# Second MLP products of six hidden blocks in sixteen as seven block products in place of eight (Strassen's scheme), weights staged in half pieces

## The chip, the cores and the metric

The kernel runs on one core of a Trainium2 chip. The metric is the device time of one execution in microseconds (us), the median of several runs. Engines are named as in the profile: PE (TensorE) multiplies, PEld loads the matrix that stands still into it, DVE (VectorE) and ACT (ScalarE) do arithmetic, POOL (GpSimd) and SP (SyncE) here mostly start DMAs or idle.

## The reference

A decoder trunk of two layers on 256 tokens of width 1024, float32 in and out. Layer 0 has stick-breaking attention, layer 1 native sparse attention with keys and values from the stream after layer 0; each is followed by a squared-ReLU MLP with a hidden width of 4096, and at the end stands an RMSNorm.

```python
def sqrelu_mlp(x, w1, w2):
    h = jax.nn.relu(x @ w1)
    return (h * h) @ w2
...
for layer in range(DEPTH):
    hn = rms_norm(h, norm_gain[layer, 0])
    ... # attention, added to h
    h = h + sqrelu_mlp(rms_norm(h, norm_gain[layer, 1]), mlp_w1[layer], mlp_w2[layer])
return rms_norm(h, final_norm)
```

## The kernel before

**Precision.** Every product of float32 numbers is made of three: each operand is split into a high part (fp32r, a cast) and a low part (the number less its high part), and high by high, high by low and low by high are added up in PSUM. `mm3` (L361) issues the three matmuls, `mm` (L355) one of them. For weights ACT makes the high part `wh` (L301) and DVE the low part `wl` (L307), in `split`.

**Weights.** All weights come in one fixed list, `feed` (L205) and `feed_mlp` (L214), in pieces of 128x2048 (1 MB), into three raw buffers. `fetch` (L255) issues a piece's DMA on SP as soon as a buffer's last reader, DVE's `wl`, is placed. Each piece is split in two halves of 1024 columns into one of three pairs wh, wl. `W` asks for a piece, `gone` gives it back.

**The MLP** (`mlp`, L465) cuts the hidden width of 4096 into 16 blocks of 256, one piece of w1 and one of w2 each. The hidden tile of a block stands with the hidden numbers on the partitions, so it has four quarters of 128x128: two halves f of the hidden numbers by two halves t of the tokens.
- First product (`first`): for each f, eight matmuls of 512 columns (wh against the tokens' high and low parts side by side) and eight of 256 (wl against the high part), into a PSUM bank `pu`. ACT copies the 256 columns of the cross product out (`mr`, L507), DVE adds the other 256 (`mu`, L508).
- `square`: DVE makes relu(u) u (`ms`, L520), ACT its high part `hh` (L521), DVE its low part `hl` (L522).
- Second product (`second`, `piece`): for each of the two column halves n of the output and the two token halves t, two quarters by three matmuls of 512 columns, which add to one of four banks `acc` over all 16 blocks. Eight products of a quarter with a 128x512 piece of w2 a block, thus 24 matmuls.

The second products of block c - 2 follow the first products of block c. Two pairs of `pu` banks alternate, so eight banks are in use: four acc, four pu. The last two blocks are worked off by (t, n) instead; as each output quarter ends, DVE scales it and adds it to the residual `hres` (`res`, L451 and L453), and `finish` (L1421) squares, scales (ACT L1433, DVE L1435), applies the gain (L1440) and writes it out (L1436). The order of (t, n) in layer 1 is (0,0), (0,1), (1,0), (1,1), and the very last quarter is done in two parts of 256 columns, the second into a bank of its own, `accz`.

**The order of work** is not written down by hand. PE's order follows the program, and a planner (`Order`, L41, with `Chain`) keeps a clock by cost formulas (`act` L159, `dve` L163, `pool` L167) and a rank for each chain of steps; ACT's and DVE's instructions are placed where their engine would be free by that clock, so that each engine then works through its own fixed list.

Of the kernel before, what the change touches and what calls it, by code (L numbers as in the profile page):

```python
# [8 lines left out]
F32 = mybir.dt.float32  # L9
# [6 lines left out]
P = 128  # L16
# [11 lines left out]
V_CUT = ((1, 1), (2, 1), (3, 1), (4, 2), (6, 2))  # L28
# [92 lines left out]
class Chain:  # L121
# [29 lines left out]
    def hurry(self):  # L151
        if self.rank > 0:
            for x in self.o.ready:
                if x[3] == self.one:
                    x[0] = 0
            self.rank = 0
# [15 lines left out]
def hybrid_kernel(ctx, tc, x, xt, eye, gcols, gfin, wqk, wv, wo0, wkv, wvs, wq, wg, wo1, w1, w2, cw1, cw2, cpos, gate_b, consts, out):  # L172
# [29 lines left out]
    NB = 3  # L202
    stream = []

    def feed(src, n, whole=False):  # L205
        stream.append((src, n, whole))
        return len(stream) - 1

    i_v0 = [feed(wv[:, n * 512:(n + 1) * 512], 512) for n in range(2)]
    i_v = [feed(wv[:, k * D:(k + m) * D], m * D) for k, m in V_CUT]  # L210
    i_qk = [feed(wqk[p], 2048) for p in range(NP)]
    i_o0 = [[feed(wo0[n, i], 2048) for n in range(2)] for i in range(2)]

    def feed_mlp(layer):  # L214
        wa, wb = [], []
        for c in range(NFC):
            wa.append(feed(w1[layer, c], 2048))
            if c >= 2:
                wb.append(feed(w2[layer, c - 2], 2048))
        return wa, wb + [feed(w2[layer, c], 2048) for c in (NFC - 2, NFC - 1)]  # L220

    i_m = [feed_mlp(0)]
    i_kv = [[feed(wkv[n, i], 2048) for i in range(2)] for n in range(2)]
# [3 lines left out]
    def feed_cw(n):  # L227
        c, i = divmod(n, 2)
        i_c[c][i] = feed(cw1[c, i], 2048, True)

    feed_cw(0)
    i_q.append(feed(wq[0], 2048))
    feed_cw(1)
    feed_cw(2)
    i_q.append(feed(wq[1], 2048))
    feed_cw(3)
    i_vs.append(feed(wvs[0], 2048))
    i_q.append(feed(wq[2], 2048))
    i_vs.append(feed(wvs[1], 2048))
    i_q.append(feed(wq[3], 2048))  # L240
    i_o1 = [[feed(wo1[n, i], 2048) for n in range(2)] for i in range(2)]
    i_m.append(feed_mlp(1))

    class Weights:
        raws, made, parts, gone, cur, landed, path, pool = [], [], [], 0, -1, 0.0, 0.0, None

    ws = Weights()
    ways = {"hi": "A"}

# [5 lines left out]
    def fetch():  # L255
        j = len(ws.raws)
        if j == len(stream):
            return
        src, n, whole = stream[j]
        if j in i_v0 or j in i_v:  # L260
            raw = ws.pool.tile([P, n], F32, name=f"rv{j}", bufs=1)
        else:
            raw = wp.tile([P, n], F32, tag="raw", name="raw", bufs=3)
        ws.raws.append(raw)
        ws.made.append(None)
        cuts = 2 if j in (0, 2) or j in i_v[-2:] else 1
# [3 lines left out]
        for h in range(2):  # L270
            if h < cuts:
                lands(P * n * 4 // cuts)
            ws.parts.append(Chain(o, whole_part(j, h) if whole else split(j, h), rank_of(j), ws.landed))

    def rank_of(j):
        return (0.5, 2, 4)[min(2, max(0, j - ws.cur))]

    def whole_part(j, half):
        if 2 * j + half:
            yield ws.his[2 * j + half - 1]  # L280
        ws.his[2 * j + half].finish()

    def split(j, half):
        n = stream[j][1]
        if 2 * j + half:
            yield ws.his[2 * j + half - 1]
        before = [i for i in range(j) if not stream[i][2]]
        while len(before) >= NB and ws.gone <= before[-NB]:
            w = Waiter()
            ws.waiting.append(w)  # L290
            yield w
        ws.parts[2 * j + half].rank = rank_of(j)
        r = slice(half * n // 2, (half + 1) * n // 2)

        def hi(e):
            def f():
                if ws.made[j] is None:
                    ws.made[j] = (wp.tile([P, n], F32R, tag="wh", name="wh", bufs=NB),
                                  wp.tile([P, n], F32R, tag="wl", name="wl", bufs=NB))
                if e == "A":  # L300
                    nc.scalar.copy(ws.made[j][0][:, r], ws.raws[j][:, r])  # L301
                else:
                    nc.vector.tensor_copy(ws.made[j][0][:, r], ws.raws[j][:, r])
            return f

        def lo():
            nc.vector.tensor_sub(ws.made[j][1][:, r], ws.raws[j][:, r], f32(ws.made[j][0][:, r]))  # L307

        m = n // 2
        k = {"A": (195 + 0.835 * m, hi("A"), False), "D": (200 + 0.49 * m, hi("D"), True)}  # L310
        yield {e: k[e] for e in ways["hi"]}
        ws.his[2 * j + half].finish()
        yield {"D": (150 + 1.045 * m, lo, True)}
        if half and j > i_v[-1]:
            fetch()

    class Waiter(Chain):
# [8 lines left out]
        def hurry(self):  # L326
            pass

    ws.his = [Waiter() for _ in range(2 * len(stream))]
    ws.waiting = []  # L330

    def W(i, half=None):
        ws.cur = max(ws.cur, i)
        while 2 * i + 1 >= len(ws.parts):
            o.run(o.run(o.t))
        for h in range(2) if half is None else (half,):
            for q in range(2 * i + h + 1):
                if not ws.parts[q].done:
                    ws.parts[q].hurry()
            o.need(ws.parts[2 * i + h])  # L340
        return ws.raws[i] if stream[i][2] else ws.made[i]

    def gone(i):
        assert ws.gone == i, (ws.gone, i)
        ws.gone += 1
        if stream[i][2]:
            fetch()
# [107 lines left out]
    def out_part(oT, acc, idx, n, kks, chains=(), ts=range(T)):  # L455
        for k in kks:
            i, kk = divmod(k, 4)
            w = W(idx[i][n], kk // 2)
            o.need(*chains)
            for t in ts:  # L460
                mm3(acc[n][t], tok(oT, k, t), cut(w, kk * 512, (kk + 1) * 512), k == 0, k == NK - 1)
# [3 lines left out]
    def mlp(layer, gi, x_, ch, pt, rs, pus, accs, mid, ends, ap):  # L465

        wa, wb = i_m[layer]
        acc = [[None, None], [None, None]]
        held = []
        r2 = [None, None]  # L470

        def piece(c, hT, t, n, q=(0, 512)):
            o.need(hT[2])
            for f in range(2):
                w = W(wb[c], f)
                if c == 0 and f == 0:
                    acc[n][t] = B(accs[2 * n + t], f"acc{t}{n}")
                mm3(acc[n][t][:, q[0]:q[1]], tok(hT, f, t), cut(w, f * D + n * 512 + q[0], f * D + n * 512 + q[1]),
                    f == 0 and (c == 0 or q[0] > 0), c == NFC - 1 and f == 1)

        def second(c, hT):
            for n in range(2):
                for t in range(T):
                    piece(c, hT, t, n)
            gone(wb[c])

        def begin(c):
            return ([B(pus[c % 2][f], f"pu{f}") for f in range(2)],
                    [ap.tile([P, 512], F32, name=m) for m in ("mr", "mu", "ms")], [])
# [1069 lines left out]
```

## Time and profile before

| | |
|---|---|
| median of 3 runs | 619.59 us (619.07 to 620.25) |
| profiled execution | 619.5 us |
| its span in the profile | 617.7 us |
| PE busy | 609.4 us, 99% of the span |
| DVE, ACT, POOL busy | 421.0, 330.0, 40.7 us |
| bytes by DMA | 108.26 MB, mean 175 GB/s |

The profiled execution's time is its span and 1.8 us around it. A busy share says how much of the span an engine had an instruction under way; matmuls are pipelined, so their listed durations overlap and can add up to more than the stretch they fill. The chain that ended last is followed back from the last instruction, at each step to what released it.

### The profile page before, as it was taken

What the parts mean: (1) busy time and instruction counts of PE and PEld (TensorE: products, weight loads), DVE (VectorE), ACT (ScalarE), POOL (GpSimd) and SP (SyncE); (2) the same over time, 40 slices, a digit from 0 to 9 for tenths busy, and PEclk for the clock granted to TensorE, in tenths of its full rate; (3) what the DMA queues carried; (4) which work ended last, traced back from release to release, by engine and by line L of the source; (5) the groups of instructions that cost most, each with busy time, mean ns of one, the idle gap of its engine ahead of it and who ended that gap; (6) DMA issues with size and microseconds to landing.
All of it is one profiled execution on the core that took longest, in us unless ns stands there. A gap on an engine that the chain in (4) does not pass through costs nothing.

```text
span 617.7 us, 8966 instructions
## 1 busy us (share of the span) xinstructions
PE 609.4 (99%) x3580; PEld 515.1 (83%) x3580; DVE 421.0 (68%) x609; ACT 330.0 (53%) x563; POOL 40.7 (7%) x57
## 2 busy tenths in 40 slices
PE   9999999999999999999999999999999999999995
PEld 6899988888888888888887788777888888888884
DVE  6668896676656566655938999664876665566645
ACT  6757674464555444443805876553653555434432
POOL 0000000000000000000111444310000000000001
PEclk9999999999999999999999999999999999999998
DMA  8973315264555545555355525212465455554501
GB/s 323 350 294 147 137 69 204 73 240 175 198 201 204 188 164 198 200 202 197 141 200 204 205 74 202 69 69 103 146 239 189 177 204 204 179 189 179 203 1 68
DMA packets 18042, 108.26 MB, mean 175 GB/s; under 512 B 2384, under 2 KB 3664, under 8 KB 5968
## 3 DMA queue, kind: packets, MB, share of 16 engines
q1 hardware_dynamic: 17424, 107.07, 47.4%
q8 instruction: 28, 0.46, 0.3%
q10 hardware_dynamic: 576, 0.62, 0.3%
q14 instruction: 14, 0.11, 0.0%
HBM read 106.63 MB, written 1.05 MB: 174 GB/s over the span
## 4 chain that ended last, share of the span: by engine, by line
PE 95%; DMA 2%; ACT 1%; issue 1%; DVE 1%; POOL 0%; POOLq 0%; DVEq 0%; ACTq 0%
PE acc L355 35%; PE pu L355 29%; PE qk L355 8%; PE pk L355 5%; PE pv L355 4%; PE po L355 3%; PE z L355 3%; PE qp L355 3%; PE ptp L367 2%; DMA raw<-in_wq 1%; PE ph L355 1%; PE pt L367 1%; PE pa L367 1%; DMA xraw<-in_xt 1%; ACT pe L1093 0%
## 5 line engine op out<-in xcount | busy, mean ns | idle before, releaser
L307 DVE TENSOR_TENSOR wl<-raw,wh 128x1024 fp32r<-128x1024 f32 x180 | 216.1, 1221 | 105.0 <-ACT wh L301 105.0
L301 ACT CAST wh<-raw 128x1024 fp32r<-128x1024 f32 x180 | 184.7, 1052 | 108.4 <-PE acc L355 45.9
L355 PE MATMUL pu<-xn,wh 128*128 128x512 f32 x512 | 129.7, 392 | 0.0
L355 PEld LDWEIGHTS pu<-xn,wh 128*128 128x128 f32 x512 | 93.3, 188 | 18.0 <-issue 0.5
L355 PE MATMUL acc<-wh,hh 128*128 128x512 f32 (+1 forms) x256 | 99.8, 390 | 0.0
L355 PE MATMUL acc<-wl,hh 128*128 128x512 f32 (+1 forms) x256 | 99.7, 390 | 0.0
L355 PE MATMUL acc<-wh,hl 128*128 128x512 f32 (+1 forms) x256 | 99.4, 388 | 0.0
L355 PEld LDWEIGHTS pu<-xn,wl 128*128 128x128 f32 x512 | 70.9, 190 | 5.7
L355 PE MATMUL pu<-xn,wl 128*128 128x256 f32 x512 | 72.6, 282 | 0.0
L355 PEld LDWEIGHTS acc<-wh,hl 128*128 128x128 f32 x256 | 48.1, 188 | 10.1
L355 PEld LDWEIGHTS acc<-wh,hh 128*128 128x128 f32 x256 | 48.2, 188 | 9.2
L355 PEld LDWEIGHTS acc<-wl,hh 128*128 128x128 f32 x256 | 48.2, 188 | 8.8
L521 ACT CAST hh<-ms 128x512 fp32r<-128x512 f32 x32 | 19.9, 621 | 61.3 <-DVE ms L520 61.3
L355 PE MATMUL qk<-xa,wh 128*128 128x256 f32 x256 | 47.3, 286 | 0.0
L355 PE MATMUL acc<-wh,oT 128*128 128x512 f32 x128 | 43.6, 403 | 0.0
L355 PEld LDWEIGHTS qk<-xa,wh 128*128 128x128 f32 x256 | 39.8, 192 | 0.5 <-issue 0.3
L507 ACT COPY mr<-pu 128x256 f32<-128x256 f32 x64 | 23.6, 369 | 23.8 <-PE pu L355 23.8
L355 PE MATMUL qk<-xa,wl 128*128 128x256 f32 x128 | 36.2, 283 | 0.0
L522 DVE TENSOR_TENSOR hl<-ms,hh 128x512 fp32r<-128x512 f32 x32 | 22.1, 691 | 19.4 <-ACT hh L521 19.4
L355 PE MATMUL pk<-wh,xk 128*128 128x512 f32 (+1 forms) x128 | 33.6, 342 | 0.0
L1093 ACT ACTIVATE pe<-z,nm 128x256 f32<-128x256 f32 (+1 forms) x64 | 26.2, 427 | 10.7 <-DVE nm L1099 10.7
L355 PEld LDWEIGHTS acc<-wh,oT 128*128 128x128 f32 x128 | 24.0, 188 | 5.6 <-issue 0.7
(181 smaller groups left out, 750.9 us busy)
## 6 DMA issues: line engine op xcount, KB each, us to landing
raw<-in_w SPq DMA_DIRECT2D x64, 1024.0 KB, 4.8
raw<-in_wqk SPq DMA_DIRECT2D x8, 1024.0 KB, 4.9
raw<-in_wo SPq DMA_DIRECT2D x8, 1024.0 KB, 4.8
raw<-in_wkv SPq DMA_DIRECT2D x4, 1024.0 KB, 4.8
raw<-in_cw SPq DMA_DIRECT2D x4, 1024.0 KB, 5.0
raw<-in_wq SPq DMA_DIRECT2D x4, 1024.0 KB, 5.4
rv<-in_wv SPq DMA_DIRECT2D x6, 512.0 KB, 7.5
raw<-in_wvs SPq DMA_DIRECT2D x2, 1024.0 KB, 5.2
```

Of the source, the lines that this page charges most:

```text
L301: nc.scalar.copy(ws.made[j][0][:, r], ws.raws[j][:, r])
L307: nc.vector.tensor_sub(ws.made[j][1][:, r], ws.raws[j][:, r], f32(ws.made[j][0][:, r]))
L355: nc.tensor.matmul(o_, a, b, start=first, stop=last, skip_group_check=True)
L367: nc.tensor.transpose(o_, a, i)
L507: yield act(256, lambda: nc.scalar.copy(r[:, q], pu[f][:, 256:512]))
L521: yield act(512, lambda: nc.scalar.copy(hh, sv))
L522: yield dve(512, lambda: nc.vector.tensor_sub(hl, sv, f32(hh)), port=True)
L1093: return act(n, lambda: nc.scalar.activation(d, z, AF.Exp, bias=nm[:, i:i + 1], accum_out=rs[:, t, hd, b:b + 1]), 150)
```

## The change

In blocks 2, 4, 6, 8, 10 and 12 of both layers (`FAST`) the second product is a 2x2 block product by Strassen's scheme: seven products of 128x512, each of three matmuls, in place of eight. They add to seven banks: four that stay the outputs' own, to which the plain blocks add as well, and three more for products 1, 6 and 7. In return the other blocks use the same four outputs by changed terms: the bank of output (t=0, n=1) holds the difference to another output (quarters E2 and S3), and product 5's bank is added to two outputs at the end. What comes with it:

- Sums of quarters of the hidden tile (E2, S1 to S4), on DVE; `hh` and `hl` then hold six or eight quarters. Sums of weights (`ty`, kinds "a" and "b"), made by DVE from two raw half pieces; ACT makes their high part `th` and DVE their low part `tl`.
- Weight pieces are halves: 128x1024 (512 KB), in six raw buffers and six pairs wh, wl, and four pairs th, tl. w1 and w2 are laid out by halves in memory (`first`, `second` in the layout function).
- Three acc banks more leave one pu bank from block 4 on: both halves of every first product use it in turn. ACT copies all 512 columns out of it (`mu`, L630 after), and DVE adds the two parts in one instruction from there (`ms`, L645). The last block's second half uses product 7's bank, which is empty again by then.
- After block 12 `gather` adds the three extra banks to `hres`: two copies on ACT, two sums and four updates on DVE.
- From block 4 to 14 the two halves of a second product stand apart: first product half 0, second product half 0 (products 1, 3, 5, 7), first product half 1, second product half 1 (products 2, 6, 4).
- The last two blocks run in the order (0,0), (1,0), (1,1), (0,1) in layer 0 and (0,0), (1,1), (0,1), (1,0) in layer 1.

```diff
-V_CUT = ((1, 1), (2, 1), (3, 1), (4, 2), (6, 2))
+FAST = ((2, 4, 6, 8, 10, 12),) * 2
...
-    NB = 3
+    H = 1024
+    NR, NB, NT = 6, 6, 4
...
+        def two(c, wide):
+            s = [w2[layer, c][:, h * H:(h + 1) * H] for h in range(2)]
+            fast = c in FAST[layer]
+            x = feed(s[0], H)
+            if fast:
+                loads.append((s[1], H, 1, False))
+                ls = [len(loads) - 2, len(loads) - 1]
+                a = item("a", H, ls)
+            if wide:
+                one(c + 2, 1)
+            if fast:
+                y = item("w", 512, ls[1:])
+                wb.append([x, y, a, item("b", H, ls)])
+            else:
+                wb.append([x, feed(s[1], H)])
...
+            yield dve(H, lambda: nc.vector.tensor_add(
+                ty, x.rearrange("p (a q) -> p a q", a=2), y[:, 512:H][:, None, :].to_broadcast([P, 2, 512])), port=True)
+        else:
...
+            yield dve(512, lambda: nc.vector.tensor_add(ty[:, 0], t0[:, 1], x[:, 0:512]), port=True)
+            yield dve(512, lambda: nc.vector.tensor_add(ty[:, 1], ty[:, 0], y[:, 0:512]), port=True)
...
+        ws.made[i] = hi, lo = [ws.tp.tile([P, H], F32R, name=t, bufs=NT) for t in ("th", "tl")]
+        yield cast(H, hi, ty)
+        ws.his[off].finish()
+        yield {"D": (150 + 1.045 * H, lambda: nc.vector.tensor_sub(lo, ty, f32(hi)), True)}
...
+        banks = {1: extra[0], 2: accs[0], 3: accs[2], 4: accs[1], 5: accs[3], 6: extra[1], 7: extra[2]}
...
+        def half(c, hT, h):
+            if c in fast:
+                x, y, a, b = wb[c]
+                if h == 0:
+                    term(1, hT, A11, x, 0)
+                    term(3, hT, S4, x, 1)
+                    gone(x)
+                    term(5, hT, S1, a, 0)
+                    term(7, hT, S3, a, 1)
+                    gone(a)
+                else:
+                    term(2, hT, A12, y, 0)
+                    gone(y)
+                    term(6, hT, S2, b, 0)
+                    term(4, hT, A22, b, 1)
+                    gone(b)
+            else:
+                for a, m, n in ((A11, 2, 0), (A21, 4, 0), (A22, 5, 1), (E2, 3, 1)) if h == 0 else (
+                        (A12, 2, 0), (A22, 4, 0), (A21, 5, 1), (S3, 3, 1)):
+                    term(m, hT, a, wb[c][h], n)
+                gone(wb[c][h])
...
+            if k0 == 0 and c >= 4:
+                if free[0] is not None:
+                    o.need(free[0])
+                pu[f] = B(extra[2] if f and c == NFC - 1 else pus[1][1], "pu")
...
-                    yield act(256, lambda: nc.scalar.copy(r[:, q], pu[f][:, 256:512]))
-                    yield dve(256, lambda: nc.vector.tensor_add(u[:, q], pu[f][:, 0:256], r[:, q]))
+                    yield act(512, lambda: nc.scalar.copy(u[:, f, :], pu[f]))
...
+                yield dve(512, lambda: nc.vector.tensor_add(s4, u4[:, :, 0], u4[:, :, 1]), port=True)
...
+                yield dve(256, lambda: nc.vector.tensor_sub(s[:, 4:6], s[:, 2::-2], s[:, 3:0:-2]), port=True)
+                if c in fast:
+                    yield dve(256, lambda: nc.vector.tensor_sub(s[:, 6:8], s[:, 1:5:3], s[:, 3:6:2]), port=True)
+                    yield dve(128, lambda: nc.vector.tensor_sub(s[:, 8], s[:, 6], s[:, 0]), port=True)
+                    yield from parts(5, 9, 4)
...
+            apart = 4 <= c < NFC - 1
+            first(c, st, 0, 0, NK)
+            if apart:
+                half(*held[0], 0)
+            first(c, st, 1, 0, NK)
+            held.append((c, square(c, st)))
+            if not apart:
+                half(*held[0], 0)
+            half(*held.pop(0), 1)
```

On PE a block of layer 0's MLP before: the first product in two banks, then 24 matmuls into the four acc banks (the first three are shown).

```order
L355 MATMUL pu0_1513<-xn_1169,wh_1432 128x512 x8
L355 MATMUL pu0_1513<-xn_1169,wl_1433 128x256 x8
L355 MATMUL pu1_1514<-xn_1169,wh_1432 128x512 x8
L355 MATMUL pu1_1514<-xn_1169,wl_1433 128x256 x8
L355 MATMUL acc00_1387<-wh_1476,hh_1382 128x512
L355 MATMUL acc00_1387<-wl_1477,hh_1382 128x512
L355 MATMUL acc00_1387<-wh_1476,hl_1383 128x512
```

On PE the second half of a first product and of a fast block's second product after it, in the same layer: one bank `pu` (2089, then 2131 for the next half), and nine matmuls between.

```order
L443 MATMUL pu_2089<-xn_1235,wh_1962 128x512 x8
L443 MATMUL pu_2089<-xn_1235,wl_1963 128x256 x8
L443 MATMUL acc2_1469<-wh_1979,hh_1912 128x512
L443 MATMUL acc2_1469<-wl_1980,hh_1912 128x512
L443 MATMUL acc2_1469<-wh_1979,hl_1913 128x512
L443 MATMUL acc6_1702<-th_2028,hh_1912 128x512
L443 MATMUL acc6_1702<-tl_2029,hh_1912 128x512
L443 MATMUL acc6_1702<-th_2028,hl_1913 128x512
L443 MATMUL acc4_1476<-th_2028,hh_1912 128x512
L443 MATMUL acc4_1476<-tl_2029,hh_1912 128x512
L443 MATMUL acc4_1476<-th_2028,hl_1913 128x512
L443 MATMUL pu_2131<-xn_1235,wh_2040 128x512 x8
```

What moved: the next first product's half now follows after nine matmuls into other banks and takes the bank that the last one filled; `th` and `tl` are the weight sums' parts.

On ACT around a block of layer 0 before: the copies out of PSUM (`mr`), the weight casts and the cast of the hidden tile.

```order
L301 CAST wh_1962<-raw_1860 128x1024 x2
L507 COPY mr_1959<-pu0_1957 128x256
L301 CAST wh_2006<-raw_1904 128x1024
L507 COPY mr_1959<-pu1_1958 128x256
L301 CAST wh_2006<-raw_1904 128x1024
L521 CAST hh_2004<-ms_1961 128x512
```

On ACT after, around the same place on PE: `mu_1271<-pu_2089` is the copy that empties the bank before pu_2131 can be filled.

```order
L630 COPY mu_1271<-pu_2034 128x512
L356 CAST wh_2068<-raw_1936 128x1024
L356 CAST wh_2081<-raw_2022 128x1024
L356 CAST wh_2113<-raw_2024 128x1024
L630 COPY mu_1271<-pu_2089 128x512
L356 CAST wh_2122<-raw_2026 128x1024
L356 CAST th_2148<-ty_2138 128x1024
L630 COPY mu_1271<-pu_2131 128x512
L650 CAST hh_2111<-ms_2033 128x512
```

What moved: a cast of a weight half (`wh_2113`) still stands right ahead of a copy, but what the copy sets free is now the only bank. 

On DVE the kernel's end before, from the last whole quarter's update of hres to the last scaling.

```order
L1440 SCALAR_TENSOR_TENSOR ys0_4112<-hres0_72,gf_4108 128x512
L453 SCALAR_TENSOR_TENSOR hres1_73<-acc10_4312,r2_4720,hres1_73 128x512
L1435 TENSOR_SCALAR ys0_4112<-ys0_4112,ssq0_4110 128x704
L1440 SCALAR_TENSOR_TENSOR ys1_4113<-hres1_73,gf_4108 128x512
L1451 TENSOR_SCALAR ssq1_4111<-ssq1_4111 128x1
L453 SCALAR_TENSOR_TENSOR hres1_73<-acc11_4331,r2_4720,hres1_73 128x256 x2
L453 SCALAR_TENSOR_TENSOR hres1_73<-accz_5531,r2_4720,hres1_73 128x256
L1451 TENSOR_SCALAR ssq1_4111<-ssq1_4111 128x1
L1440 SCALAR_TENSOR_TENSOR ys1_4113<-hres1_73,gf_4108 128x256
L1451 TENSOR_SCALAR ssq1_4111<-ssq1_4111 128x1
L1440 SCALAR_TENSOR_TENSOR ys1_4113<-hres1_73,gf_4108 128x256
L1435 TENSOR_SCALAR ys1_4113<-ys1_4113,ssq1_4111 128x704
```

On DVE the same end after.

```order
L541 SCALAR_TENSOR_TENSOR hres0_72<-acc3_4675,r2_4935,hres0_72 128x512
L1634 TENSOR_SCALAR ssq0_4452<-ssq0_4452 128x1
L541 SCALAR_TENSOR_TENSOR hres1_73<-acc4_4664,r2_4993,hres1_73 128x256
L1622 SCALAR_TENSOR_TENSOR ys_4454<-hres0_72,gf_4450 128x512
L541 SCALAR_TENSOR_TENSOR hres1_73<-acc4_4664,r2_4993,hres1_73 128x256
L1617 TENSOR_SCALAR ys_4454<-ys_4454,ssq0_4452 128x704
L541 SCALAR_TENSOR_TENSOR hres1_73<-accz_6067,r2_4993,hres1_73 128x256
L1634 TENSOR_SCALAR ssq1_4453<-ssq1_4453 128x1
L1622 SCALAR_TENSOR_TENSOR ys_4454<-hres1_73,gf_4450 128x256
L1634 TENSOR_SCALAR ssq1_4453<-ssq1_4453 128x1
L1622 SCALAR_TENSOR_TENSOR ys_4454<-hres1_73,gf_4450 128x256
L1617 TENSOR_SCALAR ys_4454<-ys_4454,ssq1_4453 128x704
```

What moved: token half 0's gain and scaling (`ys<-hres0`) now stand between the updates of the last quarter; before, that half was through ahead of them.

## Rows read from the trace of the kernel before

**Rows 1.** The page of the profile, busy time, share of the span and count of each engine, and the shares of the span by engine in the chain that ended last.

```profile
PE 609.4 (99%) x3580; PEld 515.1 (83%) x3580; DVE 421.0 (68%) x609; ACT 330.0 (53%) x563; POOL 40.7 (7%) x57
...
PE 95%; DMA 2%; ACT 1%; issue 1%; DVE 1%; POOL 0%; POOLq 0%; DVEq 0%; ACTq 0%
```

**Rows 2.** The chain that ended last in order of time, inside the first MLP. Columns: start in us from the span's start, duration in us, engine, tile written, line, count.

```profile
154.61 5.47 PE acc L355 x24
160.08 5.56 PE pu L355 x32
165.64 5.47 PE acc L355 x24
```

**Rows 3.** The table by stretches. Columns: the stretch in us, its length, then for PE, PEld, DVE, ACT and POOL the busy time (and instructions), the granted clock of PE as a share of full speed, the mean busy share of the DMA engines, GB/s. The first two are most of the first and of the second MLP, the third two whole blocks.

```profile
154.60:275.90 121.30, 121.30 (x618) 103.66 (x617) 74.12 (x92) 59.75 (x82) 0.00 (x0) 1.00 0.54 191
451.00:594.40 143.40, 143.40 (x730) 122.55 (x729) 88.03 (x109) 70.28 (x96) 0.00 (x0) 1.00 0.51 184
206.97:229.03 22.06, 22.06 (x113) 18.85 (x113) 13.37 (x17) 10.53 (x14) 0.00 (x0) 1.00 0.54 191
```

**Rows 4.** The timeline of PE over one first product. Columns: start, duration, engine, line, operation, tiles out<-in, shape, count.

```profile
137.86 1.98 PE L355 MATMUL pu<-xn,wh 128*128 128x512 f32 x8
139.68 1.11 PE L355 MATMUL pu<-xn,wl 128*128 128x256 f32 x8
140.63 2.00 PE L355 MATMUL pu<-xn,wh 128*128 128x512 f32 x8
142.47 1.12 PE L355 MATMUL pu<-xn,wl 128*128 128x256 f32 x8
...
143.42 0.40 PE L355 MATMUL acc<-wh,hh 128*128 128x512 f32 x1
```

**Rows 5.** The timeline of DVE in the first MLP. Columns as above, and in brackets the idle time ahead of an instruction and what ended it.

```profile
127.42 0.68 DVE L520 SCALAR_TENSOR_TENSOR ms<-mu 128x512 f32<-128x512 f32 x1
128.02 0.74 DVE L508 TENSOR_TENSOR mu<-pu,mr 128x256 f32<-128x256 f32 x2
...
205.35 2.36 DVE L307 TENSOR_TENSOR wl<-raw,wh 128x1024 fp32r<-128x1024 f32 x2 [1.75 <-ACT wh L301]
...
211.09 0.42 DVE L508 TENSOR_TENSOR mu<-pu,mr 128x256 f32<-128x256 f32 x1
211.43 1.22 DVE L307 TENSOR_TENSOR wl<-raw,wh 128x1024 fp32r<-128x1024 f32 x1
212.56 0.69 DVE L520 SCALAR_TENSOR_TENSOR ms<-mu 128x512 f32<-128x512 f32 x1
...
213.94 0.69 DVE L522 TENSOR_TENSOR hl<-ms,hh 128x512 fp32r<-128x512 f32 x1 [0.69 <-ACT hh L521]
```

**Rows 6.** ACT: the timeline in the first MLP; then, from the groups of instructions by line and shape, the copies of 512 columns out of PSUM (busy us, mean ns of one; idle us ahead and what ended it); then the timeline of one such copy and of the matmul that it let start.

```profile
140.88 0.37 ACT L507 COPY mr<-pu 128x256 f32<-128x256 f32 x1 [0.78 <-PE pu L355]
...
142.71 1.05 ACT L301 CAST wh<-raw 128x1024 fp32r<-128x1024 f32 x1 [1.46 <-PE pu L355]
143.67 0.37 ACT L507 COPY mr<-pu 128x256 f32<-128x256 f32 x1
...
147.17 0.62 ACT L521 CAST hh<-ms 128x512 fp32r<-128x512 f32 x1 [2.19 <-DVE ms L520]
...
L1146 ACT COPY pT<-ptp 128x512 f32<-128x512 f32 x12 | 7.1, 594 | 1.8 <-PE ptp L367 1.7
...
348.07 0.60 ACT L1146 COPY pT<-ptp 128x512 f32<-128x512 f32 x1
...
348.73 0.66 PE L367 MATMUL ptp<-ident,pe 128*128 128x128 f32 x4 [0.28 <-ACT pT L1146]
```

**Rows 7.** DMA: the stretch at the kernel's start, in columns as in the table by stretches above; the page's DMA issues (count, KB each, median us from issue to landing); and the issuing instructions of the weights' tile on SP (shortest, median and longest ns, first and last start in us).

```profile
0.00:27.40 27.40, 26.47 (x110) 19.92 (x111) 16.71 (x30) 17.46 (x26) 2.33 (x12) 1.00 0.93 356
...
raw<-in_w SPq DMA_DIRECT2D x64, 1024.0 KB, 4.8
...
raw<-in_wq SPq DMA_DIRECT2D x4, 1024.0 KB, 5.4
...
L269 SPq DMA_DIRECT2D raw<-in_w x64: 327/328/328, 85.1 to 581.3; - x64
```

**Rows 8.** The timeline of the kernel's end, DVE, PE and the last DMA issue on ACT's queue.

```profile
605.32 0.75 DVE L453 SCALAR_TENSOR_TENSOR hres<-acc,r,hres 128x512 f32<-128x512 f32 x1 [1.03 <-PE acc L355]
...
608.71 0.58 DVE L1435 TENSOR_SCALAR ys<-ys,ssq 128x704 f32<-128x704 f32 x1
...
609.20 0.68 DVE L1440 SCALAR_TENSOR_TENSOR ys<-hres,gf 128x512 f32<-128x512 f32 x1
...
610.12 0.88 DVE L453 SCALAR_TENSOR_TENSOR hres<-acc,r,hres 128x256 f32<-128x256 f32 x2
...
610.51 0.28 PE L355 MATMUL accz<-wh,hl 128*128 128x256 f32 x1
...
611.10 0.48 DVE L453 SCALAR_TENSOR_TENSOR hres<-accz,r,hres 128x256 f32<-128x256 f32 x1
...
613.14 0.59 DVE L1435 TENSOR_SCALAR ys<-ys,ssq 128x704 f32<-128x704 f32 x1 [0.44 <-POOL ssq L1454]
...
613.74 0.38 ACTq L1436 DMA_DIRECT2D out<-ys  x1
```

More of the change, by code (lines that the diff above doesn't have):

```diff
@@ L269, in fetch, with pump, used, rank_of @@
             nc.sync.dma_start(raw[:, r], src[:, r])
[L270 to L288, printed above, removed]
+            lands(P * n * 4 // cuts)
+            got.append(ws.landed)
+        ws.lands.append(got)
+        for i in range(len(items)):
+            kind, n, ls, parts, off = items[i]
+            if ls[-1] == l:
+                f = {"w": split, "r": whole_part, "a": sums, "b": sums}[kind]
+                ws.parts[i] = [None] * parts
+                for p in range(parts):
+                    ws.parts[i][p] = Chain(o, f(i, p), rank_of(i), got[min(p, cuts - 1)])
+    def pump():
+        while ws.open and len(ws.raws) < len(loads):
+            k = ring.index(len(ws.raws))
+            if k >= NR and left[ring[k - NR]]:
+                return
+            fetch()
+    def used(l):
+        left[l] -= 1
+        if not left[l]:
+            pump()
+    def rank_of(i):
+        return (0.5, 2, 4)[min(2, max(0, i - ws.cur) // 2)]
+    def whole_part(i, p):
+        off = items[i][4]
+        if off:
+            yield ws.his[off - 1]
+        ws.his[off].finish()
+    def room(i, p):
+        off = items[i][4]
+        if off + p:
+            yield ws.his[off + p - 1]
+        while ws.gone <= before[i]:
             w = Waiter()
@@ L291, in split @@
             yield w
[L292 to L315, printed above, removed]
+        ws.parts[i][p].rank = rank_of(i)
+    def cast(m, a, b):
+        k = {"A": (195 + 0.835 * m, lambda: nc.scalar.copy(a, b), False),
+             "D": (200 + 0.49 * m, lambda: nc.vector.tensor_copy(a, b), True)}
+        return {e: k[e] for e in ways["hi"]}
@@ new lines, in split @@
+    def split(i, p):
+        kind, n, ls, parts, off = items[i]
+        yield from room(i, p)
+        m = n // parts
+        r = slice(p * m, (p + 1) * m)
+        raw = ws.raws[ls[0]][:, r]
+        if ws.made[i] is None:
+            ws.made[i] = [wp.tile([P, H], F32R, tag=t, name=t, bufs=NB) for t in ("wh", "wl")]
+        hi, lo = (x[:, r] for x in ws.made[i])
+        yield cast(m, hi, raw)
+        ws.his[off + p].finish()
+        yield {"D": (150 + 1.045 * m, lambda: nc.vector.tensor_sub(lo, raw, f32(hi)), True)}
+        used(ls[0])
@@ L467, in mlp @@
         wa, wb = i_m[layer]
-        acc = [[None, None], [None, None]]
+        fast = FAST[layer]
+        acc = {}
+        banks = {1: extra[0], 2: accs[0], 3: accs[2], 4: accs[1], 5: accs[3], 6: extra[1], 7: extra[2]}
         held = []
[L470 to L485, printed above, removed]
+        r2, rn = [None, None], [None, None]
+        A11, A21, A12, A22, E2, S3, S1, S4, S2 = range(9)
+        def term(m, hT, a, w, n, last=False, q=(0, 512)):
+            o.need(hT[2][a > 3])
+            new = m not in acc or q[0] > 0
+            if m not in acc:
+                acc[m] = B(banks[m], f"acc{m}")
+            a = hT[3][a] * P
+            b = cut(W(w), n * 512 + q[0], n * 512 + q[1])
+            if q[0] > 0:
+                new = q[0] not in acc
+                if new:
+                    acc[q[0]] = True
+            mm3(acc[m][:, q[0]:q[1]], (hT[0][:, a:a + P], hT[1][:, a:a + P]), b, new, last)
@@ L538, in mlp @@
+        gathered = None
         for c in range(2, NFC):
[L539 to L540 removed]
+            if c == 5:
+                scaled = go(scales(), 3)
             st = begin(c)
[L542 to L547 removed]
@@ L644, in layer0 @@
         v_first(1)
-        v_proj(0)
-        v_proj(1)
-        v_proj(2)
-        v_proj(3)
-        v_proj(4)
+        for k in range(1, NK):
+            v_proj(k)
         o.need(*rc)
```

372 lines of the change are left out of this document (234 added, 138 removed).

## The prediction

> **What bounds the kernel now.** Read first the page's busy shares and its chain [rows 1]: PE is busy in 99% of the span, and 95% of the chain that ended last is PE. Then the chain in order of time [rows 2]: inside an MLP it is nothing but PE, first products (pu) for 5.56 us, second products (acc) for 5.47 us, again and again, so that a block of the hidden layer costs 11.03 us and two blocks 22.06. The table by stretches [rows 3] says the same of both MLPs: PE busy without a gap, granted clock 1.00 (the 2.4 GHz level), DVE at 61%, ACT at 49%. So a matmul taken away is time taken away, as long as ACT and DVE, which get new work, stay ahead of PE. What one matmul costs is its distance to the next, not its busy time, which overlaps: 24 second products in 5.47 us [rows 2] are 0.228 us each, where the trace lists some 0.40 [rows 4].
>
> **What the change takes away.** In six blocks of sixteen the second product of a block has seven products of 128x512 instead of eight, each of three matmuls (high by high, high by low, low by high). That is 3 x 6 x 2 layers = 36 matmuls of 512 columns, and PE's order shows just these missing: 726 second products of 512 columns instead of 762, all else on PE unchanged in number and, outside the MLPs, in order. 36 x 0.228 = **-8.2 us**. A fast block followed by a plain one, a pair from here on, then has 4 x 2.78 + (12 + 9 + 24) x 0.228 = 21.38 us of PE work.
>
> **What it adds on DVE.** DVE's price is the step from start to start where it works without waiting [rows 5]: 1.14 us for 1024 columns (2.36 - 1.22), 0.60 for 512, 0.34 for 256; for 128 I put 0.21, an estimate from the last two. A pair has ten instructions of 1024 (seven low parts of half pieces, two low parts of weight sums, one sum), ten of 512 (y's low part, two sums, seven on the hidden tile), four of 256, one of 128: 11.4 + 6.0 + 1.36 + 0.21 = 18.97 us. With every instruction at its whole duration (1.22, 0.69, 0.42, 0.28) it would be 21.1. Both lie under PE's 21.38, the first with 2.4 us to spare, where today it is 13.4 in 22.06 [rows 3]. A fast block by itself has 12 us of DVE work against 10.3 of PE, but weights are prepared up to six half pieces and two pairs of sums ahead, so the pair is what counts. I take no stall (0), and at the other end the rival below.
>
> **On ACT** a pair has nine casts of 1024, eight copies or casts of 512 and one of 256, at whole durations [rows 6] 9 x 1.05 + 8 x 0.62 + 0.37 = 14.8 us in 21.38. Its share is no bound; its order is, at one place.
>
> **The single bank for first products** (from block 4 on). The next first product may start when ACT has copied the last one out of PSUM. After the second half of a fast block only nine matmuls lie between: 9 x 0.228 = 2.05 us. ACT has a weight cast in front of the copy there, and that cast waits for the same matmul. From the first of the nine: ACT starts 0.25 later (140.63 to 140.88 [rows 4, 6]), the copy starts 0.96 after the cast (142.71 to 143.67), takes 0.59, and PE follows an ACT copy after 0.06 (348.67 to 348.73) [rows 6]. That is 1.86, against 2.05 less the weight load that would like to go ahead. So it is late by 0 to 0.2 us, in 12 blocks 0 to 2.4; since 1.86 is nearer to just in time, I take 0.05 each, **+0.6**. The other three copies of a pair have 2.74 us and nothing that waits in front of them for long: 0. The Trainium skill, page "Perfetto Trace Analysis", section "Optimizing Tensor Performance", says that independent matmul groups should rotate through different PSUM banks, so that emptying one overlaps the next group; it speaks against this change, and by it, with no group of another bank between, each emptying would be exposed. With the rows' 0.25 + 0.59 + 0.06 = 0.9 us for two halves of eleven blocks in two layers that would be 40 us; that would be some 652 in all, and I give it 1 in 100, inside the first rival's chance, since PE's order puts nine or twelve matmuls into other banks behind each half.
>
> **The last block of each layer.** Before block 15's hidden tile is ready, DVE has, from the end of block 14's first product, 17 instructions: four of 1024, seven of 512, two of 256 and four updates of hres (0.75 whole [rows 8], so some 0.67 from start to start, an estimate): 4.56 + 4.20 + 0.68 + 2.68 = 12.1 us. It starts 1.3 later (ACT's copy first), the cast of the hidden tile (0.62 [rows 6] and its start) adds 0.7, together 14.1. PE comes there after 2.05 + 5.56 + 5.47 + 1.37 = 14.45. With DVE's whole durations it would be 1.4 later, 1.0 behind PE. So 0 to 1 in each layer, I take 0.1 each: **+0.2**.
>
> **The end of the kernel** gets longer. Today the first token half is finished two quarters of the last products before the end, now one, because the order is (0,0), (1,1), (0,1), (1,0). Last matmul at L = 610.51 [rows 8]: DVE took the first quarter-tile at L - 0.39, and the last at L + 0.59. Now DVE's order has the other half's gain (0.60), one more quarter (0.35) and the scaling of 704 columns (0.5 of its 0.58) between: L - 0.39 + 0.34 + 0.60 + 0.35 + 0.50 = L + 1.40. After it stands the same chain as today. **+0.8**, bounds 0.3 and 1.2.
>
> **Moved, at no cost.** Weight pieces are halved: SP has 94 more issues of 0.33 us each on a queue that mostly waits for buffers, one 1 MB piece landing 4.8 us after its issue [rows 7]. Eight half pieces in 21.38 us have that time with two under way, even if a half took the full 4.8 (8 x 4.8 / 2 = 19.2). If a half took 5.4, as the longer row, 21.6: 0.2 x 12 = 2.6 us. I take 0, since in the first stretch pieces of 512 KB and less came at 356 GB/s [rows 7], and the MLPs need 191 [rows 3]. Attention and NSA have the same PE order, with ACT's and DVE's orders locally changed; PE is dense there too: 0, bounds -0.6 and +1. The gather of the three extra banks (two copies on ACT, two sums and four updates on DVE) falls into blocks 14 and 15 and is in the count above.
>
> **Sum** against the profiled execution's 619.5 us (median of the runs 619.59, so the two agree): 619.5 - 8.2 + 0.6 + 0.2 + 0.8 = **612.9 us**. Low end: no bank wait, tail +0.3, -0.6 elsewhere: 611.0. High end of this case: 2.4 + 1.0 + 1.2 against the full 8.2: about 616.
>
> **Rivals.**
> *Emptying the bank comes late.* If in the 12 fast blocks another cast of 0.95 slips between the matmul's end and the copy, or its semaphore comes by so much later, 1.86 + 0.95 = 2.81 against some 1.94: 0.87 x 12 = 10.4, and 612.3 (the sum without its 0.6) becomes 622.7, **slower**. It decides from 0.6 us a block on, (8.2 - 0.8 - 0.2) / 12. For it: ACT works in order, and its copy stands behind a cast. Against it: that cast waits for nothing that comes after the matmul. 5%; a part of it, 0.2 to 0.5 a block (615 to 618.3), 8%.
> *DVE becomes the bound.* If the low parts wait for their casts as today's does (0.69 before hl [rows 5]), in all five of a pair: 18.97 + 3.45 = 22.42, 1.04 more than PE: 612.3 + 12.5 = 624.8, slower. From 22.0 on it is no gain. Against it: DVE's order puts other work between; for it: 89% is what it never had to do. 4%; between 21.38 and 21.85 (to 618), 6%.
> *Half pieces arrive too slowly.* As worked out, 2.6 us with two under way; 615.5. 3%. The Trainium skill, page "DMA: Bandwidth & Descriptors", section "Bandwidth", asks for at least 1 MiB in a transfer, which this change halves; the first stretch's 356 GB/s speaks against its deciding here.
> *The change doesn't do what it says:* PE's order excludes it for the 36 matmuls.
>
> **How the numbers follow.** The forecast's own case (611 to 616) has 71%; smaller gains by bank, DVE or transfers (to 618.3) 16%, a larger gain 2%, no change 3%, slower 8%. A measurement of this kernel tells some 0.2% (1.2 us) from no change, so faster, below 618.35: 0.71 + 0.16 + 0.02 = 0.89; within 0.03; slower 0.08. The range takes the first case and the nearer part of the smaller gains: 611.0 to 616.6.
>
> **What would show it.** A pair at 21.4 us in the chain (5.56 and 4.79, then 5.56 and 5.47), PE without gaps; DVE near 89% and still waiting for ACT or PE, not PE for DVE. A gap before each fast block's following pu, put down to ACT's copy, sizes the bank term; the distance from the last matmul to the last issue, 3.2 us today [rows 8], should be 4.0. Wrong would be: pairs longer than 21.6, PE's idle put down to DVE's wl or tl, or waits on raw landing.

## The result and the profile after

The changed kernel takes **615.73 us** (median of 4 runs, 615.60 to 616.42), the kernel before 619.46 beside it; the ratio is 0.994, with a 95% interval of 0.9923 to 0.9958. That is 0.6% less time, clear of no change, so faster as the prediction counts it, and inside the range of 611.0 to 616.6; but it is 3.7 us of gain where the forecast's 612.9 had 6.6. The profiled execution took 616.42 us, the longest of the four, with a span of 614.6. Ratios here and below leave out three executions of two to three and a half times the usual length, two of the kernel before and one of the run a_best9.

The page of the changed kernel, in the parts of [rows 1] and the landing times of [rows 7]:

```profile
PE 604.0 (98%) x3544; PEld 507.7 (83%) x3544; DVE 507.2 (83%) x743; ACT 377.1 (61%) x623; POOL 40.6 (7%) x57
...
PE 90%; DVE 5%; DMA 2%; ACT 1%; issue 1%; POOL 0%; SPq 0%; POOLq 0%; ACTq 0%; DVEq 0%
...
raw<-in_w SPq DMA_DIRECT2D x128, 512.0 KB, 4.8
```

PE has the 36 matmuls less (3580 to 3544) and still bounds the kernel. The chain's 5% of DVE, 1% before, stands almost whole in NSA (layer 1's sparse attention), between 340 and 388 us. Inside an MLP the chain is nothing but PE, as before; here one pair of blocks and the start of the next (columns as in [rows 2]):

```profile
160.45 2.77 PE pu L443 x16
163.22 2.77 PE acc L443 x12
165.99 2.77 PE pu L443 x16
168.76 2.77 PE acc L443 x12
171.53 2.77 PE pu L443 x16
174.30 2.79 PE acc L443 x12
177.08 2.81 PE pu L443 x16
179.89 2.09 PE acc L443 x9
181.98 2.77 PE pu L443 x16
```

A pair takes 181.98 - 160.45 = 21.53 us, not 21.38. There is no gap in it: what has grown is the step of the second products, the time from one matmul's start to the next's, 2.77 / 12 = 0.231 us and 2.09 / 9 = 0.232, against 5.47 / 24 = 0.228 [rows 2]. The table by stretches (columns as in [rows 3]) says the same of two pairs and of most of the first MLP: PE busy without a gap at a granted clock of 1.00, DVE at 38.96 / 43.07 = 90%.

```profile
160.45:203.52 43.07, 43.07 (x219) 36.55 (x219) 38.96 (x57) 29.12 (x40) 0.00 (x0) 1.00 0.57 184
149.97:285.00 135.03, 135.03 (x680) 114.31 (x680) 118.96 (x161) 85.27 (x114) 1.04 (x2) 1.00 0.60 197
```

The clearest place is the end, where both kernels run the same kind of work: twelve matmuls to a bank, little on DVE. First the kernel before, then the changed one, each from PE's timeline:

```profile
600.14 0.39 PE L355 MATMUL acc<-wh,hl 128*128 128x512 f32 x1
600.36 0.39 PE L355 MATMUL acc<-wh,hh 128*128 128x512 f32 x1
600.59 0.39 PE L355 MATMUL acc<-wl,hh 128*128 128x512 f32 x1
...
602.40 0.39 PE L355 MATMUL acc<-wh,hh 128*128 128x512 f32 x1
```

```profile
600.18 0.39 PE L443 MATMUL acc<-wh,hl 128*128 128x512 f32 x1
600.41 0.39 PE L443 MATMUL acc<-wh,hh 128*128 128x512 f32 x1
600.64 0.40 PE L443 MATMUL acc<-wl,hh 128*128 128x512 f32 x1
...
602.50 0.40 PE L443 MATMUL acc<-wh,hh 128*128 128x512 f32 x1
```

Ten steps take 2.26 us before and 2.32 after. With the trace's starts in ns, before settles to 226.7 ns after five matmuls of some 232 ns; the changed kernel never settles, and goes through sevens of 231, 231, 229, 230, 232, 241, 232, each to within 1 ns: 232.3 on average. Over the kernel (first matmul of each stage, from the two traces, us; the differences add up to -3.0, as those of the spans do):

| | before | after | difference | forecast |
|---|---|---|---|---|
| up to the first MLP | 114.73 | 115.40 | +0.67 | 0 |
| first MLP | 178.29 | 175.71 | -2.58 | -3.7 |
| NSA | 139.58 | 140.14 | +0.56 | 0 |
| second MLP, to the last matmul | 177.92 | 175.36 | -2.56 | -3.7 |
| from there to the span's end | 7.14 | 8.04 | +0.90 | +0.8 |

### The profile page after: what moved, and what is told of

Its sections match the earlier page's. It is cut to its first block, busy times and chain, and to the rows that moved or that the text cites. A ratio compares the mean times of both kernels' runs of the same rounds, so it can differ in the third digit from the quotient of the medians.

```text
span 614.6 us, 9427 instructions
## 1 busy us (share of the span) xinstructions
PE 604.0 (98%) x3544; PEld 507.7 (83%) x3544; DVE 507.2 (83%) x743; ACT 377.1 (61%) x623; POOL 40.6 (7%) x57
## 4 chain that ended last, share of the span: by engine, by line
PE 90%; DVE 5%; DMA 2%; ACT 1%; issue 1%; POOL 0%; SPq 0%; POOLq 0%; ACTq 0%; DVEq 0%
PE acc L443 35%; PE pu L443 29%; PE qk L443 8%; PE pk L443 4%; PE pv L443 3%; PE po L443 3%; PE z L443 2%; PE qp L443 2%; DVE wl L371 2%; PE ph L443 1%; DMA raw<-in_wq 1%; PE pt L455 1%; PE pa L455 1%; DMA rv<-in_wv 1%; PE ptp L455 1%
## 5 line engine op out<-in xcount | busy, mean ns | idle before, releaser
L371 DVE TENSOR_TENSOR wl<-raw,wh 128x1024 fp32r<-128x1024 f32 (+1 forms) x180 | 210.0, 1190 | 30.9 <-ACT wh L356 29.4
L356 ACT CAST wh<-raw 128x1024 fp32r<-128x1024 f32 (+1 forms) x180 | 180.2, 1025 | 63.5 <-issue 23.2
L443 PE MATMUL acc<-wh,hl 128*128 128x512 f32 x196 | 77.1, 394 | 0.0
L443 PE MATMUL acc<-wh,hh 128*128 128x512 f32 x196 | 76.9, 393 | 0.0
L443 PE MATMUL acc<-wl,hh 128*128 128x512 f32 x196 | 76.9, 392 | 0.0
L630 ACT COPY mu<-pu 128x512 f32<-128x512 f32 x64 | 37.3, 583 | 20.8 <-PE pu L443 20.8
L650 ACT CAST hh<-ms 128x512 fp32r<-128x512 f32 x64 | 34.1, 553 | 16.4 <-DVE ms L646 12.9
L443 PEld LDWEIGHTS acc<-wh,hl 128*128 128x128 f32 x196 | 36.8, 188 | 8.4
L356 ACT CAST th<-ty 128x1024 fp32r<-128x1024 f32 x24 | 25.2, 1051 | 26.2 <-DVE ty L390 13.8
L651 DVE TENSOR_TENSOR hl<-ms,hh 128x512 fp32r<-128x512 f32 x64 | 37.3, 600 | 0.2 <-ACT hh L650 0.2
```

What stands on the lines that cost most here:

```text
L356: k = {"A": (195 + 0.835 * m, lambda: nc.scalar.copy(a, b), False), "D": (200 + 0.49 * m, lambda: nc.vector.tensor_copy(a, b), True)}
L371: yield {"D": (150 + 1.045 * m, lambda: nc.vector.tensor_sub(lo, raw, f32(hi)), True)}
L443: nc.tensor.matmul(o_, a, b, start=first, stop=last, skip_group_check=True)
L630: yield act(512, lambda: nc.scalar.copy(u[:, f, :], pu[f]))
L650: yield act((b - a) * P, lambda: nc.scalar.copy(hh[:, into], flat[:, q]))
L651: yield dve((b - a) * P, lambda: nc.vector.tensor_sub(hl[:, into], flat[:, q], f32(hh[:, into])), port=True)
```

## The experiments

**Theories.** What slows the second products? A: where the hidden tile's parts lie in SBUF, the memory of the tiles. The change adds a tiny tile `rn`, one column in four buffers of 32 bytes, and the tiles of attention, NSA and the MLPs that are allocated after it begin 128 bytes further on. In the addresses of the built kernels `wh`, `wl` and the tokens' `xn` stand at 160 modulo 256 in both; `hh` and `hl` stood at 160 too and are now at 32. B: three matmuls to a PSUM bank before the next bank, where there were six. C: DVE, busy for 90%, reading SBUF beside PE. The first runs move the tiles and nothing else; each engine keeps its instructions and their order.

**Run a_pad128:** the changed kernel, put back by 128 bytes.

```diff
-        ws.tp = ap
+        ws.tp = ap; ap.tile([P, 32], F32, name="pad", bufs=1)
```

> The changed kernel with 128 unused bytes per partition ahead of the MLPs' own tiles (hidden tile, its parts, the weight sums' parts), the instructions and their order being the same. In the trace of the changed kernel a matmul of 512 columns in the second products lies 232.3 ns from the next on average, in a pattern of seven that comes back, where it settles to 226.7 ns after five in the kernel before; the first products settle in both. Theory A, the place of the hidden tile's parts in SBUF: they moved by 128 bytes against the weights (32 in place of 160 modulo 256); put back, the second products settle to 227 ns again and the time falls by about 726 x 4.5 ns = 3.3 us, to 612.5. Theory B, the runs of three matmuls to one bank before the next bank where there were six: no change, 615.7. Theory C, DVE at 83 to 89% reading SBUF beside PE: no change, 615.7.

Measured 612.41 us (612.17 to 613.02), ratio to before 0.9886 (0.9873 to 0.9899). The chain of the same pair of blocks:

```profile
164.98 2.77 PE pu L443 x16
167.75 2.75 PE acc L443 x12
...
178.78 2.07 PE acc L443 x9
180.84 2.77 PE pu L443 x16
183.61 2.75 PE acc L443 x12
186.36 2.77 PE pu L443 x16
```

The pair is 186.36 - 164.98 = 21.38 us, as forecast, and the second products settle to 227 ns. The MLPs take 174.21 and 173.84, 4.08 less than before each. Theory A stands, B and C fall: banks and DVE's load are as they were. By the medians, 3.3 us of 615.7 were the place of the MLPs' tiles; by the MLPs of the two traces, 3.0.

**Run b_pad128:** the other way round, the kernel before moved by the same line in its `mlp`.

> The kernel before with 128 unused bytes per partition ahead of the MLPs' own tiles, so that its hidden tile's parts stand where those of the changed kernel stand modulo 256. Theory A (place in SBUF): the second products go to some 232.3 ns a matmul, about 768 x 4.5 ns = 3.5 us more, 623.0. Theories B (short runs per bank) and C (DVE's load): no change, 619.5.

Measured 623.78 (623.56 to 624.39), ratio 1.0068 (1.0056 to 1.0081), with no other change than 128 unused bytes. Its chain has both products longer:

```profile
166.63 5.58 PE acc L355 x24
172.21 5.59 PE pu L355 x32
177.80 5.58 PE acc L355 x24
```

Second products 5.58 in place of 5.47 [rows 2]; the first products, 5.59 in place of 5.56, take a few matmuls more to settle after them. The pattern of the changed kernel appears, 232.3 ns.

**Runs a_pad64, a_pad256 and a_pad192:** 16, 64 and 48 columns in place of the 32.

> As the run with 128 bytes, with 64 (the hidden tile's parts at 96 modulo 256). Theory A does not say which places are good: if only the same place as the weights' modulo 256 is, this stays at 232 ns a matmul and 615.7; if every place but one is good, it falls to 227 ns and 612.5. Theories B and C: no change.

> As the run with 128 bytes, with 256 (the hidden tile's parts at 32 modulo 256 again, 288 in place of 32 modulo 512). Theory A with the place modulo 256: no change, 615.7 and 232 ns. If the place counts modulo 512 in some other way it can differ. Theories B and C: no change.

> As the run with 128 bytes, with 192 (the hidden tile's parts at 224 modulo 256, 64 ahead of the weights' place where the run with 64 bytes was 64 behind it). That run settled in a pattern of 226, 229 and 232 ns, 228.9 on average. If only the distance counts: the same pattern, 614. If the sign counts too: 227 as with 128 bytes, or 232 as in the changed kernel.

One execution each: 614.09, 615.08 and 616.78 us. Since the start of the kernel differs from one execution to the next (the first MLP begins at 114.27 to 115.40 us in the traces of the changed kernel and these four), the step of the second products in the trace tells them apart better: the last 66 matmuls of 512 columns, in ns, with the place of `hh` less that of `wh`, modulo 256:

| run | distance | step | pattern |
|---|---|---|---|
| a_pad128, before | 0 | 226.7 once settled | even |
| a_pad64 | 192 | 228.9 | 226, 229, 232 |
| a_pad192 | 64 | 233.4 | 231, 236 |
| changed kernel, a_pad256, b_pad128 | 128 | 232.3 | 231, 231, 229, 230, 232, 241, 232 |

With 256 bytes the pattern is the changed kernel's again, so the place counts modulo 256 in the one case tried. The sign counts too: 64 ahead costs 4.5 ns more than 64 behind. That a_pad64 would be either 232 or 227 was wrong, and 233.4 for a_pad192 was in none of its three cases.

**Run b_wp128:** against what does it count? The kernel before, with weights and hidden tile moved alike, and the tokens not.

```diff
-    NB = 3
+    NB = 3; wp.tile([P, 32], F32, name="pad", bufs=1)
```

> The kernel before with 128 unused bytes ahead of the weights' buffers, which moves the weights' parts and the hidden tile's parts alike (both at 32 modulo 256), while the tokens' parts stay at 160. If the place of the tile held still counts against that of the tile streamed past it: the second products stay at 227 ns a matmul (32 against 32), and the first products (tokens at 160 streamed past weights at 32) go from 228.5 to some 232, as do the attention's products of tokens and weights; 622 to 623. If the place of the tile held still counts by itself: both products slow, some 626. If the place of the streamed tile counts by itself: second products slow, first products as before, 623.

Measured 621.7 (one execution), a little under the 622 to 623 expected. Its chain:

```profile
166.55 5.46 PE acc L355 x24
172.00 5.61 PE pu L355 x32
177.62 5.46 PE acc L355 x24
183.07 5.61 PE pu L355 x32
```

Now the second products (weights streamed at 32 past a hidden tile at 32) are at their best, and the first products (tokens streamed at 160 past weights at 32) have the long step, 232.2 ns for their 512 columns; the attention's products of these tiles go to 232 and 233 as well. So it is the distance between the tile held still and the tile streamed past it.

But a matmul's own distance does not set its step alone. The parts of the weight sums, `th` and `tl`, were allocated with the hidden tile and moved with it, so for 144 of the changed kernel's 726 second products the distance is 0; yet they take 224 to 239 ns, 231.9 on average. They come six at a time behind matmuls at distance 128. In a_pad64 such six, again at distance 0, take 231, 235, 229, 232, 231 and 226 ns: the steps before a row of matmuls settles cost as much as a wrong place, and six in a row barely get through them.

**Run a_tail:** the longer end. To a_pad128, the order of quarters:

```diff
-        end = i > 1 and q[1] == 512
+        end = i % 2 == 1 and q[1] == 512
...
-    scoped(mlp, "m1", 1, 3, x1, ch, pt, rs, ((2, 3), (6, 7)), (0, 1, 4, 5), (2, 3, 6), finish, ((0, 0), (1, 1), (0, 1), (1, 0)), ends)
+    scoped(mlp, "m1", 1, 3, x1, ch, pt, rs, ((2, 3), (6, 7)), (0, 1, 4, 5), (2, 3, 6), finish, ((1, 1), (1, 0), (0, 1), (0, 0)), ends)
```

> The changed kernel with the 128 bytes, and in layer 1 the last two blocks in the order (1,1), (1,0), (0,1), (0,0), so that token half 1 is through two quarters before the end. If the longer end (8.05 us from the last matmul to the span's end against 7.14 in the kernel before) comes from the order of quarters: it goes back to some 7.15, 612.4 - 0.9 = 611.5. If it comes from what stands around it (the additional update of product 5, later scaling): no change, 612.4.

From the last matmul to the span's end it is 7.06 us, against 8.02 in a_pad128: the order of quarters explains the end. The median, 612.23 (611.65 to 613.03; ratio 0.988, 0.9866 to 0.9895), doesn't show the 0.96 clearly: the intervals of the two overlap. Of the spans, the median is 610.1 against 610.65.

**Runs a_fast1 and a_fast7:** what is a fast block worth, and when does DVE bound? a_pad128 with `FAST = ((12,),) * 2` and `FAST = ((2, 4, 5, 7, 9, 10, 12),) * 2`.

> The changed kernel with the 128 bytes and only block 12 of each layer as seven products. If a fast block is worth its three matmuls and nothing else: ten fast blocks less are 30 matmuls of 0.2285 us, 612.4 + 6.9 = 619.3. If DVE's and ACT's additional work or the weight sums cost PE time, that comes back with them: less than 6.9 slower, 617 to 618.5.

> The changed kernel with the 128 bytes and seven fast blocks of each layer, 2, 4, 5, 7, 9, 10 and 12, so that twice a fast block follows a fast one. If PE remains the bound: 6 matmuls of 0.2285 us less, 612.4 - 1.4 = 611.0. If DVE becomes it, with some 24 us of work in two fast blocks against 20.7 of PE: PE waits for weights' low parts there, up to 3 us in each place, 612.4 to 618.

619.65 us (618.96 to 620.15, ratio 0.9997, 0.9987 to 1.0007) and 611.32 (610.79 to 612.05, ratio 0.9866, 0.9851 to 0.988), each near the first case of its expectation. In the traces the first MLP takes 177.61 with one fast block, 174.21 with six and 173.53 with seven: 0.68 us a block all the way, three matmuls. Carried on to none it is 178.29, what the kernel before takes (the table above): half pieces, the single bank and the sums cost PE nothing in the MLP. With one fast block the kernel gains nothing all the same: what the MLPs save, 1.36 us, goes to the end (+0.84), to NSA (+0.3) and, in the profiled execution, to the start (+0.5).

**Runs a_best8 and a_best9:** all that helped together, a_tail with `FAST = ((2, 3, 5, 6, 8, 9, 11, 12),) * 2` and with `FAST = ((2, 3, 4, 6, 7, 8, 10, 11, 12),) * 2`.

> All that helped together: the 128 bytes, the order of quarters with the short end, and eight fast blocks of each layer (2, 3, 5, 6, 8, 9, 11, 12). Seven fast blocks took 0.68 us from each MLP against six, which is three matmuls. If PE remains the bound: 12 matmuls of 0.2285 us less than with six, and 0.99 off the end, 612.4 - 2.7 - 1.0 = 608.7. DVE was busy for 89% of the middle of an MLP with six, 94% with seven; if it becomes the bound at some 98%, because the spare time doesn't lie where it is wanted: PE waits for low parts, 609 to 613.

> The same with nine fast blocks (2, 3, 4, 6, 7, 8, 10, 11, 12). DVE's work goes up by another 4.4% of that stretch, to some 102%: it becomes the bound, PE waits for low parts, and the time is no better than with eight, 609 to 615. If DVE's instructions run closer than their listed durations and PE remains the bound: 607.3.

Eight take **609.24 us** (608.89 to 610.36), ratio to before 0.9837 (0.9824 to 0.9851), the fastest of all; nine take 625.26 (lowest 624.01), ratio 1.0087 (1.0072 to 1.0103), 10 us beyond the longest time expected. With eight the MLPs take 172.91 and 172.47, for the eighth block 0.62 and 0.69 less than with seven. The middle of the first MLP with eight, then with nine:

```profile
150.00:270.00 120.00, 120.00 (x616) 102.71 (x616) 117.56 (x160) 83.73 (x113) 0.00 (x0) 1.00 0.60 199
```

```profile
150.00:270.00 120.00, 116.65 (x591) 98.35 (x590) 113.27 (x155) 78.07 (x107) 0.00 (x0) 1.00 0.54 177
```

With eight DVE is busy for 117.56 of 120 us and PE has no gap; with nine PE idles from 251.7 us on, and PE's waits name the weights' parts:

```profile
PE acc L443 <- DVE wl L371: 5.2, 6, 2.3
PE acc L443 <- ACT th L356: 3.4, 4, 1.1
PE acc L443 <- DVE tl L397: 3.0, 4, 0.8
```

(columns: us in total, times, the longest). The first place where it idles:

```profile
251.60 1.04 ACT L356 CAST th<-ty 128x1024 fp32r<-128x1024 f32 x1 [1.79 <-DVE ty L390]
252.68 1.23 DVE L397 TENSOR_TENSOR tl<-ty,th 128x1024 fp32r<-128x1024 f32 x1 [1.11 <-ACT th L356]
252.70 0.50 PE L443 MATMUL acc<-th,hh 128*128 128x512 f32 x1 [0.65 <-ACT th L356]
253.96 0.50 PE L443 MATMUL acc<-tl,hh 128*128 128x512 f32 x1 [0.76 <-DVE tl L397]
```

ACT waits for DVE's sum, DVE for ACT's cast, and PE for both, one after the other; so DVE too is busy for less (113.27). The step from eight to nine costs 16 us where PE's work falls by 1.4. Some 1.2 us of it, in the profiled execution, are the clock: in the second MLP's last products PE waited for weights' low parts from 601.6 us on, 2.3 us and then three times for some 0.3, and after that six matmuls lie 414 to 427 ns apart, the 1.2 GHz level, in place of 227. The granted clock, third from the end of this row, is 0.80 there:

```profile
601.00:609.50 8.50, 5.91 (x18) 3.82 (x17) 7.19 (x11) 1.13 (x3) 0.00 (x0) 0.80 0.00 0
```

The nine stand in threes (2, 3, 4 and so on); another spacing of nine was not tried.

## Why the prediction was right and its size was not

**The matmuls taken away, -8.2: right.** With the tiles where they were, the MLPs take 4.08 us less each, 8.16 in all, 0.68 for every fast block.

**The step that failed is the price of those that stay.** "What one matmul costs is its distance to the next", 0.228 us, was taken from before and put unchanged on the 726 that remain. They cost 0.231 to 0.232. In the profiles that is 1.50 and 1.52 us in the MLPs (a_pad128 against the changed kernel), in the medians 615.73 - 612.41 = 3.3. The range had room above 612.9 for a late bank, a late DVE and a longer end; that this cost, which the working didn't have, fits into that room is luck. Nothing in the rows of before could show it, since there all tiles stand at the same place modulo 256; the built kernels' addresses did, and weren't compared.

**The single bank, +0.6: nothing.** The timeline of the changed kernel after a fast block's second half:

```profile
200.31 1.11 PE L443 MATMUL pu<-xn,wl 128*128 128x256 f32 x8
200.56 1.05 ACT L356 CAST wh<-raw 128x1024 fp32r<-128x1024 f32 x1 [2.12 <-issue]
201.26 0.40 PE L443 MATMUL acc<-wh,hh 128*128 128x512 f32 x1
...
201.51 0.58 ACT L630 COPY mu<-pu 128x512 f32<-128x512 f32 x1
...
203.35 1.98 PE L443 MATMUL pu<-xn,wh 128*128 128x512 f32 x8
```

The copy is through at 202.09, and PE wants the bank at 203.35: 1.26 us to spare. The working had the cast ahead of the copy wait for the bank's last matmul. It starts at 200.56, 0.7 before that half ends and 0.25 after the first matmul on `wl` starts: its buffer is the one of the `wh` that the half has just read, free ahead of the eight on `wl`. So the copy starts 0.25 after the half's end and not 1.2. To go against the rule of the Trainium skill that independent matmul groups should rotate through PSUM banks ("Perfetto Trace Analysis", "Optimizing Tensor Performance") cost nothing here, as nine matmuls into other banks cover the copy.

**The last block, +0.2: nothing that shows.** The -8.16 are 36 matmuls of 226.7 ns and leave no room for it.

**The end, +0.8: right**, +0.90, and a_tail takes it back. The last issue comes 4.17 us after the last matmul, 3.23 before [rows 8], forecast 4.0:

```profile
606.60 0.28 PE L443 MATMUL accz<-wh,hl 128*128 128x256 f32 x1
...
610.77 0.38 ACTq L1618 DMA_DIRECT2D out<-ys  x1
```

**Attention and NSA, 0 within -0.6 to +1.** NSA takes 139.90 to 139.94 us in the changed kernel's versions with unused bytes and one to eight fast blocks, 0.3 more than the 139.58 of before, and 0.56 more in the changed kernel's profile. PE has a wait there that it does not have before, for DVE's part of NSA's output, at 387.5 us and likewise in a_pad128:

```profile
PE acc L443 <- DVE oT L533: 0.5, 1, 0.5
```

So "PE is dense there too" gave no 0 once ACT's and DVE's orders had changed. NSA's own tiles lie 128 bytes further on as well; no run moved them back. The 0.67 at the start belong to that execution: PE waited there for a first weight's cast,

```profile
PE pv L443 <- ACT wh L356: 1.0, 1, 1.0
```

behind a piece that landed late, and with the same instructions a_pad128 reached the first MLP at 114.80. From the forecast's 612.9 to the profiled 616.4 it is thus +3.0 for the place, +0.7 at the start, +0.6 in NSA, +0.1 at the end, and -0.8 for the bank and the last block.

**The rivals.** DVE did not bound at 90%, and the pair's 18.97 to 21.1 us of work bracketed what it was busy for, 38.96 / 2 = 19.5. The rival is real but lies further on: between eight and nine fast blocks. The rivals' chances, as listed, add up to 9% for slower and 17% for smaller gains, where the summary has 8 and 16. Half pieces did not arrive too slowly: a half takes 4.8 us to land, as long as a whole piece did [rows 7], but it has six buffers where there were three, and PE waits for none in the MLPs. The 356 GB/s of the first stretch were no proof for small pieces, since pieces of 1 MB were issued in it too, from 15.12 us on; the changed kernel, with no piece over 512 KB, moved 354 GB/s in its first 28 us. The Trainium skill ("DMA: Bandwidth & Descriptors", "Bandwidth") asks for at least 1 MiB in a transfer to reach three quarters of the peak; with half of that the first MLP moved its 184 to 197 GB/s all the same.

## What to carry to other kernels

Where PE is the bound, a change of tiles has a price per matmul that no count of instructions shows: compare the step from start to start in the second trace before believing the count, and the addresses of the tile held still and the tile streamed, modulo 256, before the run. Here a scratch tile of a few bytes cost 3 us where the scheme that saves matmuls brought 8.2. And where one engine takes on work to relieve another, go on until the next step loses: the gain was 0.62 to 0.69 us a block up to 98% of DVE, and one block in each layer beyond that cost 16 us.

## What the runs showed of the hardware

A float32r matmul of 512 columns on a 128x128 tile, each with its own load of the tile held still, at a granted clock of 1.00 (2.4 GHz): 226.7 ns from start to start when the two tiles lie at the same place modulo 256 bytes, 228.9, 232.3 and 233.4 at distances of 192, 128 and 64 (held less streamed). The 226.7 come only after some longer steps when the matmuls before were of another kind: five of some 232 behind 256-column matmuls (before, a_pad128), seven behind second products at distance 128 (b_pad128's first products). Matmuls of 256 columns do not show it: 118.4 ns at distance 128 (b_wp128's first products) and 118.9 at 0 (before).

The Trainium skill ("TensorE: Matmul & The Clock Gate", "Step-by-step: what each phase is for") has loading the next tile take nothing from the reads of the running matmul. Here the place of the two tiles changes the step by 1 to 3%, which that sentence would not lead one to expect; whether it is these reads that meet, no run here shows. Other places than multiples of 64 bytes, and other types, were not tried.
